# Latent attention of a two-layer trunk: TensorE in program order, in slots of two score tiles, with one batch of value products per unit

## The chip, the cores and the metric

The kernel is one program on one core of a Trainium2 chip. The metric is the device time of one execution in microseconds. The engines are TensorE (PE in the rows, PEld for its weight loads), VectorE (DVE), ScalarE (ACT), GpSimd (POOL) and SyncE (SP), which issues the DMAs.

## The reference

Two layers of a trunk run for two groups of tokens with the same weights: 128 prompt tokens, which attend among themselves, and 512 sample tokens, which attend to all sample keys and 128 cached ones. Each layer modulates its input, projects it, mixes it by three kinds of heads, projects the mixture out, and ends with a gated feed-forward part. Cut to what matters:

```python
def layer(x, cond, lp, layer_idx, ctx_cache):
    mod = jax.nn.silu(cond) @ lp["w_ada"] + lp["b_ada"]
    sh1, sc1, g1, sh2, sc2, g2 = jnp.split(mod.reshape((-1, 1, mod.shape[-1])), 6, axis=-1)
    ...
    y, new_ctx = mixers(x * (1.0 + sc1) + sh1, lp, lam, lam_init, ctx_cache)
    x = layer_norm(DEEPNORM_ALPHA * x + g1 * y, lp["ln1_g"], lp["ln1_b"])
    hf = x * (1.0 + sc2) + sh2
    f = (jax.nn.silu(hf @ lp["w_ff1"]) * (hf @ lp["w_ff3"])) @ lp["w_ff2"]
    x = layer_norm(DEEPNORM_ALPHA * x + g2 * f, lp["ln2_g"], lp["ln2_b"])

# in mixers: y_a a gated convolution, y_b differential attention (4 heads, two maps each), y_c:
    cq = rms_norm(m_cq, lp["q_norm_w"]);  qc = cq @ w_uq      # 8 heads of 64 + 32 (rotary)
    ckv = rms_norm(m_ckv, lp["kv_norm_w"])                     # sample: joined with the cached keys
    kv = ckv_all @ w_ukv                                       # 8 heads of 64 key + 64 value
    sc = jnp.einsum("bhqd,bhkd->bhqk", q_m, k_m) * MLA_SCALE   # q_m, k_m: 96 wide
    o_c = jnp.einsum("bhqk,bhkd->bhqd", jax.nn.softmax(sc, axis=-1), v_m)
    y = jnp.concatenate([y_a, y_b, y_c], axis=-1) @ w_out
```

## The kernel before

All 640 tokens (256 sample, 128 prompt, 256 sample) stand side by side as columns of tiles of 128 features. Large products are split into high and low parts in fp32r (three products each, `matmul3`, L344). A layer runs `stage_in` (input projection), `attention`, `stage_residual` (output projection), `stage_ff`.

Attention for the sample tokens is planned in `plan_steps` (L1383) as 64 steps, one score tile each: 128 queries of one head (and, in differential attention, one map) against 640 keys. Four differential units of eight tiles are followed by eight latent units (`mla_unit`, two heads by two query blocks, four tiles). `scores` (L1189) makes a tile: six products for a latent one (two for a differential one) into a PSUM buffer from `mm()`, the row maximum on VectorE (L1199), the exponential with its row sum on ScalarE (L1210), then the reciprocal (VectorE, L1248) and the scaling of P (GpSimd, L1249). `av_steps` (L1262) then makes the value products of a unit over five blocks of 128 keys: `tp(kt)` transposes the unit's four P tiles on TensorE (L1270) into a PSUM tile and copies it to an SBUF tile PT (L273 on ScalarE and L275 on VectorE in turn); `av(kt)` multiplies with the values into one accumulator from `ac()` (L1281). A dict `after` holds what follows a step: `put(i, f)` appends to step i. The value steps of a unit start `LAG` steps after its last score, and each step makes the next block's transposes and this block's value products. Side work is put there in the same way, by the tables at the head: loads of a pair of heads (`LOADS`, `load_pair`), the prompt's attention (`diff_prompt`, `mla_prompt`, as generators in two parts), the norm of the differential heads (`diff_norm`, three parts), all by `SIDE`, the split of finished rows (`split_y`), and in layer 0 the products that make later modulation vectors (`ada`, L491; `ada_pe` on TensorE for the first 24 calls, then `ada_pool`; `ada_finish` transposes the sum).

Steps 0 to 31 run between the jobs of the input projection and of the latent projections (`STEPS`, `JSTEPS`). The jobs are over then, and the rest, called here the last part, runs alone: `attention` (L1452) opens the PSUM stage "tr" and calls `step(1)` until all is done. PSUM there: two score buffers of two banks (`mm`), two banks "trx" for transposes, one bank "tr", one accumulator bank "ac".

The order of the program text isn't the order on the engines. A scheduler lays out each engine's queue from the dependencies and from predicted times, and takes an instruction that it holds to be ready ahead of an earlier one that isn't, unless a hint (`issue_after`) binds it. Each engine then works its queue off in that fixed order. Tiles of a pool are given out in turn, so that a new one waits until the old user of its buffer is done.

## Time and profile before

| what | value |
|---|---|
| median of 3 runs | 1757.66 us (1756.95 to 1759.01) |
| profiled execution | 1755.1 us |
| its span, first to last instruction | 1753.3 us |
| TensorE busy | 1697.4 us, 97% of the span |
| VectorE busy | 976.3 us, 56% |
| ScalarE busy | 614.0 us, 35% |
| GpSimd busy | 248.3 us, 14% |
| mean granted TensorE clock | 0.985 |

Times in the rows are microseconds from the start of the span, unless marked ns. A line such as L1195 is a line of the kernel; `out<-in` names its tiles. Matmuls overlap, so TensorE's busy time counts some of it twice. The chain of waits goes back from the end, at each step to what released the instruction, or to the one before it on its engine.

### The profile page before, as it was taken

What the parts mean: (1) busy time and instruction counts of PE and PEld (TensorE: products, weight loads), DVE (VectorE), ACT (ScalarE), POOL (GpSimd) and SP (SyncE); (2) the same over time, 40 slices, a digit from 0 to 9 for tenths busy, and PEclk for the clock granted to TensorE, in tenths of its full rate; (3) what the DMA queues carried; (4) which work ended last, traced back from release to release, by engine and by line L of the source; (5) the groups of instructions that cost most, each with busy time, mean ns of one, the idle gap of its engine ahead of it and who ended that gap; (6) DMA issues with size and microseconds to landing.
All of it is one profiled execution on the core that took longest, in us unless ns stands there. A gap on an engine that the chain in (4) does not pass through costs nothing.

```text
span 1753.3 us, 29480 instructions
## 1 busy us (share of the span) xinstructions
PE 1697.4 (97%) x11983; PEld 1587.8 (91%) x11983; DVE 976.3 (56%) x1824; ACT 614.0 (35%) x1046; POOL 248.3 (14%) x226
## 2 busy tenths in 40 slices
PE   8999989999999999999999999899999999999997
PEld 6998867698999999999999997678999999999997
DVE  3656777747466656756476668764652232232226
ACT  1334554524431122122245546554353212212221
POOL 0011113440001010101211111232300000000014
PEclk9999989999999999999999999899999999999998
DMA  9665584421354545545314634622212222222211
GB/s 335 207 200 142 170 253 130 127 84 55 103 148 148 156 132 147 172 128 151 103 52 142 218 121 158 179 73 78 73 61 75 82 73 73 69 79 82 68 53 60
DMA packets 100871, 217.38 MB, mean 124 GB/s; under 512 B 12160, under 2 KB 28928, under 8 KB 100736
## 3 DMA queue, kind: packets, MB, share of 16 engines
q1 hardware_dynamic: 100736, 215.50, 39.4%
q8 instruction: 94, 1.54, 0.4%
q14 instruction: 41, 0.34, 0.1%
HBM read 185.28 MB, written 30.18 MB: 123 GB/s over the span
## 4 chain that ended last, share of the span: by engine, by line
PE 85%; DVE 6%; DMA 3%; ACT 3%; issue 2%; SPq 0%; POOL 0%; POOLq 0%; ACTq 0%; DVEq 0%
PE mm L349 61%; PE mm L1195 4%; PE mm L372 4%; PE ac L1281 3%; PE mm L1514 3%; PE trx L1270 3%; PE mm L995 1%; DMA rawt<-in_w_ada 1%; PE mm L401 1%; DVE wu L140 1%; ACT hv L782 1%; DMA raw<-in_w_ada 1%; PE tr L449 1%; DMA mk<-kd 1%; ACT wu L138 1%
## 5 line engine op out<-in xcount | busy, mean ns | idle before, releaser
L349 PE MATMUL mm<-h,wu 128*128 128x384 f32 (+1 forms) x4944 | 736.0, 310 | 1.8 <-ACT kp L909 1.5
L349 PEld LDWEIGHTS mm<-h,wu 128*128 128x128 f32 x4944 | 724.7, 188 | 8.8 <-issue 5.4
L138 ACT CAST wu<-stg 128x1024 fp32r<-128x1024 f32 (+2 forms) x200 | 201.6, 1011 | 686.7 <-PE mm L349 334.1
L140 DVE TENSOR_TENSOR wu<-stg,wu 128x1024 fp32r<-128x1024 f32 (+2 forms) x200 | 239.4, 1200 | 157.5 <-ACT wu L138 155.2
L349 PE MATMUL mm<-gh,wu 128*128 128x256 f32 (+1 forms) x1184 | 258.7, 309 | 0.0
L349 PEld LDWEIGHTS mm<-gh,wu 128*128 128x128 f32 x1184 | 198.7, 188 | 0.9 <-issue 0.6
L349 PE MATMUL mm<-gl,wu 128*128 128x384 f32 (+1 forms) x592 | 182.8, 309 | 0.0
L1199 DVE TENSOR_REDUCE nm<-mm 128x1 f32<-128x640 f32 x128 | 104.8, 818 | 50.9 <-PE mm L1195 50.1
L1548 DVE TENSOR_TENSOR gs<-gs,mm 128x640 f32<-128x640 f32 (+2 forms) x48 | 36.6, 763 | 149.1 <-PE mm L349 149.1
L668 DVE SCALAR_TENSOR_TENSOR x<-mm,ga,x 128x512 f32<-128x512 f32 x48 | 36.0, 750 | 144.8 <-PE mm L349 144.8
L349 PEld LDWEIGHTS mm<-gl,wu 128*128 128x128 f32 x592 | 111.4, 188 | 0.2 <-issue 0.2
L527 DVE SCALAR_TENSOR_TENSOR acc<-rawt,scT,acc 128x512 f32<-128x512 f32 x98 | 75.6, 772 | 58.7 <-DMA rawt<-in_w_ada 57.5
L372 PE MATMUL mm<-h,wu 128*128 128x384 f32 (+1 forms) x576 | 98.1, 327 | 7.6 <-ACT h L783 6.9
L372 PEld LDWEIGHTS mm<-h,wu 128*128 128x128 f32 x576 | 90.7, 201 | 12.7 <-ACT h L783 9.6
L349 PE MATMUL mm<-hi,wu 128*128 128x384 f32 (+1 forms) x400 | 89.9, 311 | 0.1
L687 POOL TENSOR_TENSOR accS<-x 128x640 f32<-128x640 f32 x4 | 9.9, 2480 | 506.3 <-DVE x L674 506.3
L1195 PE MATMUL mm<-mk,mq 96*128 96x384 f32 (+1 forms) x384 | 74.9, 336 | 5.7 <-ACT P L1210 2.3
L532 DVE SCALAR_TENSOR_TENSOR rawt<-rawt,scT 128x512 f32<-128x512 f32 x98 | 74.8, 763 | 2.1 <-POOL rawt L525 2.1
L1195 PEld LDWEIGHTS mm<-mk,mq 96*128 96x128 f32 x384 | 63.7, 200 | 12.7 <-ACT P L1210 4.9
L349 PEld LDWEIGHTS mm<-hi,wu 128*128 128x128 f32 x400 | 67.9, 188 | 2.6 <-issue 1.5
L1210 ACT ACTIVATE P<-mm,nm 128x640 f32<-128x640 f32 x56 | 44.6, 796 | 57.1 <-DVE nm L1199 44.7
L525 POOL TENSOR_SCALAR acc<-rawt,scT 128x512 f32<-128x512 f32 x14 | 9.8, 697 | 373.7 <-PE tr L542 373.6
(272 smaller groups left out, 2250.2 us busy)
## 6 DMA issues: line engine op xcount, KB each, us to landing
stg<-in_w_ff SPq DMA_DIRECT2D x104, 512.0 KB, 3.6
rawt<-in_w_ada SPq DMA_DIRECT2D x160, 256.0 KB, 3.0
stg<-in_w_in SPq DMA_DIRECT2D x30, 512.0 KB, 4.2
stg<-in_w_ff SPq DMA_DIRECT2D x32, 448.0 KB, 3.3
raw<-in_w_ada SPq DMA_DIRECT2D x32, 256.0 KB, 6.2
stg<-in_w_out SPq DMA_DIRECT2D x16, 512.0 KB, 4.4
mk<-kd SPq DMA_DIRECT2D x32, 240.0 KB, 5.9
mq<-qd SPq DMA_DIRECT2D x32, 192.0 KB, 5.4
```

The costliest lines, as they stand in the source:

```text
L138: nc.scalar.copy(u[:, 0, :ncol], t[:, :ncol])
L140: (nc.gpsimd if self.lo_pool else nc.vector).tensor_sub(u[:, 1, :ncol], t[:, :ncol], u[:, 0, :ncol].bitcast(F32))
L349: self.last = nc.tensor.matmul(out, w(k, pw), x(k, px), start=(k == 0 and i == 0), stop=(k == nk - 1 and i == 2)).ins
L372: self.last = nc.tensor.matmul(ps, u[:, pw, 128 * k:128 * k + 128], x(k, px)[:, c0:c1], start=(k == 0 and i == 0), stop=(k == NK - 1 and i ...
L527: nc.vector.scalar_tensor_tensor(self.acc[0], w, c[0], self.acc[0], ALU.mult, ALU.add)
L532: nc.vector.scalar_tensor_tensor(self.acc[1], w, c[1], self.acc[1], ALU.mult, ALU.add)
L1195: nc.tensor.matmul(ps[:, 128 + c0:128 + c1], q[:96, qc:qc + 128], k[:96, c0:c1], start=(i == 0), stop=(i == len(pairs) - 1))
L1199: nc.vector.tensor_reduce(nm, s, axis=AX.X, op=ALU.max, negate=True)
L1210: self.exp_end = nc.scalar.activation(P, s, AF.Exp, bias=nm, accum_out=sm).ins
L1270: nc.tensor.transpose(p[:, 256 * i + 128 * q:256 * i + 128 * q + 128], tiles[i, q][:, 128 * kt:128 * kt + 128], self.ident)
L1281: nc.tensor.matmul(acc[64 * i:64 * i + 64, :256], v(kt, i), hold[kt][:, 256 * i:256 * i + 256], start=(kt == 0), stop=(kt == 4))
L1514: self.last = self.nc.tensor.matmul(ps[:, c0:c1], u[:, pw, 128 * k:128 * k + 128], x(k, px)[:, c0:c1], start=(k == 0 and j == 0), stop=(k ...
```

## The change

- From the stage "tr" on, TensorE's instructions are chained in the order of the program text: `in_order` binds each one to the one traced before it (an order, not a wait for its end).
- Steps run in slots: `slot` traces two score steps and then the side work put at either.
- From the last differential unit on, a unit's value products are one batch: transposes of blocks 0 and 1, then 2 and 3, then 4, at 2, 3 and 4 steps after its last score, and all value products at 5 steps. Before, they were five mixed steps from 4 steps on. For the earlier units the mixed steps stay, some one step earlier. Where no more `ada_pe` calls come, block 4 of a batch goes to the bank "tr".
- PT has six buffers instead of three.
- The prompt's parts are three instead of two (`prompt_out` yields before its value products), at new steps. Their scores and value products, and the scale product of `diff_norm`, go to the accumulator bank (its last block to "tr") instead of a score buffer.
- The prompt's operands (`p32`) are loaded by a step of their own, into one buffer instead of two.
- The `ada` calls stand at listed steps, and in this stage `ada_finish` follows two steps later.

The diff, with hunks of mere bookkeeping left out:

```diff
--- before.py
+++ after.py
...
@@ -56,8 +56,11 @@
 ADV = 0
 HOLD = 2
 LOADS = (29, 37, 43, 52)
-SIDE = ((34, 37), (37, 40, 43), (36, 40), (47, 50, 56), (44, 47), (49, 51), (51, 54), (60, 62))
-ADA_N = 12
+P32 = (38, 45, 49, 54)
+NPT = 6
+SIDE = ((32, 36, 38), (40, 43, 47), (36, 40, 42), (44, 47, 57), (44, 48, 50), (48, 52, 54), (52, 56, 58),
+        (60, 64, 66))
+ADA_AT = (32, 34, 38, 42, 44, 46, 50, 54, 58, 60, 62, 66)
 ADA_IN = 1
 ADA_PE = 6
 ADA_OUT = 2
@@ -315,6 +318,20 @@
             self.defer(n, fn)
         else:
             fn()
+
+    @contextmanager
+    def in_order(self):
+
+        traced, prev = self.nc.cur_bb.bb.instructions, self.pe_end
+        n = len(traced)
+        yield
+        for i in traced[n:]:
+            if i.engine == self.nc.tensor.engine:
+                if prev is not None:
+                    self.tc.add_manual_dep(i, prev.name, mybir.DependencyInfo(mybir.DependencyClass.NoSync,
+                                                                              mybir.DependencyReason.DATA))
+                prev = i
+        self.pe_end = prev
 
     def tick(self):
         for x in self.later:
@@ -510,7 +527,9 @@
             nc.vector.tensor_copy(self.ada_part, ps[:, :128])
         else:
             nc.vector.tensor_add(self.ada_part, ps[:, :128], self.ada_part)
-        if q == 3:
+        if q == 3 and self.kind == "tr":
+            self.after.setdefault(self.g + 2, []).append(lambda acc=self.ada_part: self.ada_finish(acc, key))
+        elif q == 3:
             self.ada_finish(self.ada_part, key)
 
     def ada_pool(self, key, q):
@@ -1183,8 +1202,11 @@
                 self.move(q[part][:96, :512], self.qd[r, :, part, :].rearrange("r i c -> (r i) c"))
                 self.move(k[part][:96, :], self.kd[r, :, part, :].rearrange("r i c -> (r i) c"))
             self.mq[h], self.mk[h] = q, k
-        self.p32[p] = self.at.tile([96, 2, 2, 128], F32, tag="p32", name="p32", bufs=2)
-        nc.sync.dma_start(self.p32[p], self.pd[64 * p:64 * p + 64].rearrange("(h r) i a c -> (r i) h a c", h=2))
+
+    def load_p32(self, p):
+
+        self.p32[p] = self.at.tile([96, 2, 2, 128], F32, tag="p32", name="p32", bufs=1)
+        self.nc.sync.dma_start(self.p32[p], self.pd[64 * p:64 * p + 64].rearrange("(h r) i a c -> (r i) h a c", h=2))
 
     def scores(self, pairs, qc):
 
@@ -1212,7 +1234,7 @@
 
     def pt(self):
         if self.at:
-            return self.at.tile([128, 512], F32, tag="PT", name="PT", bufs=3)
+            return self.at.tile([128, 512], F32, tag="PT", name="PT", bufs=NPT)
         return self.t(name="PTt")[:, 0:512]
 
     def diff_unit(self, l, p, hf):
@@ -1259,12 +1281,14 @@
             self.ys[2 + p] = self.t(name="yo")
         return self.ys[2 + p]
 
-    def av_steps(self, tiles, v, dst, hf):
+    def av_steps(self, tiles, v, dst, hf, batch):
+
+
         nc = self.nc
         hold = {}
 
         def tp(kt):
-            p = self.tr(True)
+            p = self.tr(not batch or kt < 4 or self.ada_i < 4 * ADA_PE)
             for i in range(2):
                 for q in range(2):
                     nc.tensor.transpose(p[:, 256 * i + 128 * q:256 * i + 128 * q + 128],
@@ -1291,6 +1315,9 @@
                 tp(kt + 1)
             av(kt)
 
+        if batch:
+            return [lambda kts=kts: [tp(kt) for kt in kts] for kts in ((0, 1), (2, 3), (4,))] + \
+                [lambda: [av(kt) for kt in range(5)]]
         return [lambda kt=kt: step(kt) for kt in range(5)]
 
     def soft_prompt(self, ps, n, neg=None):
@@ -1318,7 +1345,8 @@
         nc.tensor.transpose(p[:, 128:256], Pb, self.ident)
         pt = self.pt()
         self.copy(pt[:, :256], p[:, :256])
-        acc = p[:, 256:384]
+        yield
+        acc = self.ac()[:, 0:128]
         for i in range(2):
             nc.tensor.matmul(acc[64 * i:64 * i + 64, :], v(i), pt[:, 128 * i:128 * i + 128], start=True, stop=True)
         self.copy(dst[:, 256:384], acc)
@@ -1329,26 +1357,26 @@
         kv = km.rearrange("p (g t) -> p g t", g=4)
         nc.vector.tensor_mul(kv, self.kp32[:, p, :].unsqueeze(1).to_broadcast([128, 4, 128]),
                              self.block4.unsqueeze(2).to_broadcast([128, 4, 128]))
-        ps = self.mm()
+        ps = self.ac()
         nc.tensor.matmul(ps[:, :512], self.qp32[:, p, :], km, start=True, stop=True)
         P, Pv = self.soft_prompt(ps, 4, self.neglam[:, l:l + 1])
         yield
         h = Pv.rearrange("p (a b) t -> p a b t", b=2)
         nc.vector.tensor_add(h[:, :, 0, :], h[:, :, 0, :], h[:, :, 1, :])
-        self.prompt_out(P[:, 0:128], P[:, 256:384],
-                        lambda i: self.dvp[:, 128 * p + 64 * i:128 * p + 64 * i + 64], self.ob(p))
+        yield from self.prompt_out(P[:, 0:128], P[:, 256:384],
+                                   lambda i: self.dvp[:, 128 * p + 64 * i:128 * p + 64 * i + 64], self.ob(p))
         yield
 
     def mla_prompt(self, l, p):
         nc = self.nc
         x = self.p32[p]
-        ps = self.mm()
+        ps = self.ac()
         for i in range(2):
             nc.tensor.matmul(ps[:, 128 * i:128 * i + 128], x[:, i, 0, :], x[:, i, 1, :], start=True, stop=True)
         P, Pv = self.soft_prompt(ps, 2)
         yield
-        self.prompt_out(P[:, 0:128], P[:, 128:256],
-                        lambda i: self.vmp[:, 64 * (2 * p + i):64 * (2 * p + i) + 64], self.ob(2 + p))
+        yield from self.prompt_out(P[:, 0:128], P[:, 128:256],
+                                   lambda i: self.vmp[:, 64 * (2 * p + i):64 * (2 * p + i) + 64], self.ob(2 + p))
         yield
 
     def diff_norm(self, l, p):
@@ -1364,13 +1392,14 @@
         nc.vector.tensor_scalar(v, ps[:, :10], 1.0 / 64, 1e-6, ALU.mult, ALU.add)
         y = self.newton(v, 10)
         yield
-        pm = self.mm()
-        for j in range(5):
-            for i in range(2):
-                nc.tensor.matmul(pm[64 * i:64 * i + 64, 128 + 128 * j:256 + 128 * j],
-                                 y[:, 2 * j + i:2 * j + i + 1].to_broadcast([128, 64]), self.ident,
-                                 start=True, stop=True)
-        nc.vector.scalar_tensor_tensor(ob, ob, self.col("diff", l, 0), pm[:, 128:768], ALU.mult, ALU.mult)
+        for pm, j0, j1 in ((self.ac(), 0, 4), (self.tr(), 4, 5)):
+            for j in range(j0, j1):
+                for i in range(2):
+                    nc.tensor.matmul(pm[64 * i:64 * i + 64, 128 * (j - j0):128 * (j - j0) + 128],
+                                     y[:, 2 * j + i:2 * j + i + 1].to_broadcast([128, 64]), self.ident,
+                                     start=True, stop=True)
+            o = ob[:, 128 * j0:128 * j1]
+            nc.vector.scalar_tensor_tensor(o, o, self.col("diff", l, 0), pm[:, :128 * (j1 - j0)], ALU.mult, ALU.mult)
         yield
 
     def load_y(self, m):
@@ -1404,6 +1433,9 @@
         def unit(kind, p, hf, n):
             hold = {}
             g0 = len(self.steps)
+            end = g0 + n - 1
+            batch = end >= 31
+            at = (end + 2, end + 3, end + 4, end + 5) if batch else [end + LAG + (n * kt) // 6 for kt in range(5)]
 
             def start():
                 hold["u"] = kind(l, p, hf)
@@ -1416,12 +1448,12 @@
             def av(kt):
                 if kt == 0:
                     _, tiles, v, dst = hold["u"]
-                    hold["av"] = self.av_steps(tiles, v, dst, hf)
+                    hold["av"] = self.av_steps(tiles, v, dst, hf, batch)
                 hold["av"][kt]()
             for i in range(n):
                 self.steps.append(lambda i=i: step(i))
-            for kt in range(5):
-                put(g0 + n - 1 + LAG + (n * kt) // 5, lambda kt=kt: av(kt))
+            for kt, i in enumerate(at):
+                put(i, lambda kt=kt: av(kt))
 
         for kind, p, hf in units:
             unit(kind, p, hf, 8 if kind == self.diff_unit else 4)
@@ -1429,6 +1461,8 @@
             put(i, lambda g=g: self.assemble_diff(1, 2 * g, 2 * g + 2))
         for p, i in enumerate(LOADS):
             put(i, lambda p=p: self.load_pair(p))
+        for p, i in enumerate(P32):
+            put(i, lambda p=p: self.load_p32(p))
         parts(lambda: self.diff_prompt(l, 0), *SIDE[0])
         parts(lambda: self.diff_norm(l, 0), *SIDE[1])
         parts(lambda: self.diff_prompt(l, 1), *SIDE[2])
@@ -1438,8 +1472,8 @@
         put(54, lambda: self.load_y(0), lambda: self.load_y(1))
         for i, j in enumerate((58, 59, 56, 57, 58, 62)):
             put(j, lambda i=i: self.split_y(i))
-        for i in range(ADA_N):
-            put(32 + 2 * i, lambda: self.ada(1))
+        for i in ADA_AT:
+            put(i, lambda: self.ada(1))
 
     def step(self, n):
         for _ in range(n):
@@ -1448,6 +1482,16 @@
             for f in self.after.pop(self.g, []):
                 f()
             self.g += 1
+
+    def slot(self):
+
+        g = self.g
+        for f in self.steps[g:g + 2]:
+            f()
+        for i in (g, g + 1):
+            for f in self.after.pop(i, []):
+                f()
+        self.g += 2
 
     def attention(self, l):
         pool = self.tc.tile_pool(name="at", bufs=1, reuse_waits="tile")
@@ -1470,8 +1514,10 @@
             self.tick()
         self.W.lo_pool = False
         self.stage("tr")
+        self.pe_end = None
         while self.g < len(self.steps) or self.after:
-            self.step(1)
+            with self.in_order():
+                self.slot()
         self.split_y(6)
         self.split_y(7)
         self.stage("any")
```

## Rows read from the trace of the kernel before

**Rows 1.** The page, part 1: busy time, share of the span, instructions.

```profile
PE 1697.4 (97%) x11983; PEld 1587.8 (91%) x11983; DVE 976.3 (56%) x1824; ACT 614.0 (35%) x1046; POOL 248.3 (14%) x226
```

**Rows 2.** Busy time by stretch: PE, PEld, DVE, ACT, POOL; granted clock; DMA share, GB/s.

```profile
1107.30:1204.10 96.80, 93.10 (x662) 67.38 (x662) 65.72 (x152) 52.93 (x113) 34.31 (x40) 0.98 0.36 107
...
249.40:257.00 7.60, 6.61 (x34) 4.21 (x34) 2.47 (x6) 2.13 (x5) 1.60 (x2) 0.50 1.03 337
257.00:353.90 96.90, 94.19 (x773) 66.53 (x771) 69.82 (x168) 51.52 (x109) 35.67 (x40) 1.00 0.44 132
```

**Rows 3.** The chain of waits, layer 1: start, length, what; a score to value products.

```profile
1179.29 1.77 PE mm L1195 x12
1181.07 0.44 PE trx L1270 x4
1181.51 1.01 PE ac L1281 x8
1182.52 0.59 PE trx L1270 x4
...
1184.00 0.58 PE ac L1281 x4
```

**Rows 4.** Who waited for whom, layer 1, weight loads: in total, times, longest.

```profile
PEld trx L1270 <- issue: 13.5, 35, 0.4
```

**Rows 5.** The chain of waits, layer 1, pieces in its breaks.

```profile
1112.44 0.89 ACT P L1210 x2
...
1196.09 0.81 DVE lo L838
...
1197.14 0.81 POOL Pc L1249
...
1202.79 0.59 ACT PT L273
```

**Rows 6.** The chain of waits, layer 0: breaks, and one group of modulation products.

```profile
255.78 0.83 DVE nm L1199
...
295.57 0.57 PE tr L449 x16
...
318.62 2.79 DMA rawt<-in_w_ada
...
352.58 0.59 ACT PT L273
```

**Rows 7.** TensorE in order of time, layer 0: modulation products; idle before, releaser.

```profile
239.29 0.64 PE L449 MATMUL tr<-rawt,scT 128*32 128x128 f32 x16
...
251.98 0.65 PE L449 MATMUL tr<-rawt,scT 128*32 128x128 f32 x8 [0.99 <-DMA rawt<-in_w_ada]
```

**Rows 8.** The chain of waits, layer 1: prompt and norm work.

```profile
1118.91 0.87 PE mm L1333 x2
...
1122.48 0.37 PE tr L1323 x4
...
1156.23 0.45 PE mm L1347 x4
...
1157.84 1.01 PE tr L1362 x10
...
1175.87 1.24 PE mm L1370 x20
```

**Rows 9.** VectorE, layer 1, by line: busy us, mean ns, idle before, releasers.

```profile
L1199 DVE TENSOR_REDUCE nm<-mm 128x1 f32<-128x640 f32 x31 | 25.3, 817 | 5.6 <-PE mm L1195 5.1
L275 DVE COPY PT<-trx 128x512 f32<-128x512 f32 x18 | 12.4, 687 | 3.3 <-PE trx L1270 2.8 <-PE tr L1318 0.4
...
L275 DVE COPY yo<-ac 128x256 f32<-128x256 f32 x8 | 3.4, 425 | 4.0 <-PE ac L1281 3.9
```

**Rows 10.** The line that loads p32: issues on SP in ns, time to landing.

```profile
L1187 SPq DMA_DIRECT2D p<-pd x8: 317/327/414, 235.3 to 1156.7; - x8
...
DMA to landing us min/median/max: 2.4/2.9/6.7
```

More of the change, by code (lines that the diff above doesn't have):

```diff
@@ L1 @@
 import math
-from contextlib import ExitStack, nullcontext
+from contextlib import ExitStack, contextmanager, nullcontext
 import numpy as np
```

## The prediction

> **What bounds the kernel now.** I read the page first: TensorE is busy for 1697.4 of 1753.3 us [rows 1], so only what TensorE does, or waits for, can move the end. The change touches the latent part of attention, so I cut out of each layer the stretch in which that part runs alone: in layer 1 from the end of the second latent score tile (1108.96) to the first product of the output projection (1204.08), 95.1 us; in layer 0 from 249.5 to 353.9, 104.4 us. VectorE is busy for two thirds to three quarters of both, ScalarE for a little over half [rows 2]; TensorE bounds. By its busy time there seem to be only 3.7 us of headroom in layer 1. That time counts overlapping instructions, so I then read the chain of waits, which gives each piece once. There two score tiles of six products take 1.77 us, one block of four transposes 0.44 us behind scores but 0.59 us behind value products, and two value steps 1.01 us together but one alone 0.58 us [rows 3]. So going from transposes to value products costs 0.15 us, and the way back 0.16 us. The list of waits shows the latter from the side of the weight loads: 35 times a transpose's weights come late, with no releaser [rows 4].
>
> Then the breaks, where the chain leaves TensorE. Layer 1 has six (1.8, 1.6, 1.9, 1.1, 2.5 and 0.7 us), the first with the exponential at 1112.44, the longest with a split on VectorE at 1196.09 and GpSimd at 1197.14, the last with ScalarE's copy at 1202.79 [rows 5]; together 9.6. Each of the first four stands behind a prompt score or a norm's scale product, which had taken one of the two score buffers, so that the next score waited for the only other one's exponential. Layer 0 has six as well (1.8, 1.6, 1.9, 3.8, 2.5, 0.7), from the reduction at 255.78 to the copy at 352.58, with the one around the DMA of modulation weights at 318.62 [rows 6], plus 1.0 us of waiting for such weights at 251.98 [rows 7]; together 13.3.
>
> The work of layer 1 without changes of kind: 30 scores x 0.88 = 26.4; 45 transpose blocks x 0.43 = 19.4; 45 value steps x 0.43 = 19.4 [rows 3]; prompts and norms 2 x 0.87 + 4 x 0.45 + 12 x 0.11 + 6 x 0.37 + 2 x (1.01 + 1.24) = 11.6 [rows 8]; 0.7 for eight transposes at the lower clock. That is 77.5. The chain spends 95.1 - 9.6 = 85.5 on TensorE; the 8.0 left are the changes of kind (35 x 0.16 = 5.6 into transposes, the rest into value products).
>
> The Trainium skill ("Perfetto Trace Analysis", Identifying the Most-Contended Engine) says that TensorE's matmul busy share is no measure of headroom. By the busy share, 93.10 of 96.80 us [rows 2], this change could give 3.7 us there at most; by the chain 9.6 + 8.0. I go by the chain.
>
> **The change, part by part.**
>
> *One batch of value products per unit.* Per unit the sequence becomes transposes (2), (2), (1), then five value steps in a row. With nine such batches a layer (eight latent units and the last differential one) 9 x 0.15 + 9 x 0.16 = 2.8 us of changes stand where 8.0 stood: -5.2 us a layer, on the path, as TensorE bounds. The five transposed tiles of a unit now live at once, which six PT buffers hold; the prompt's masked keys take the next one and wait for the first value step, which comes early in a batch of 2.3 us.
>
> *Slots and program order.* Two score tiles, then the side work of two steps, and nothing of the stretch may pass: behind a waiting instruction stands everything that TensorE has here, and all other engines wait for that. A score buffer comes free 0.82 (reduction) + 0.89 (exponential and its sum) + some 0.2 of handovers = 1.9 us after its score ends [rows 5, 9]. A slot with value products covers this (2.3 + 1.0); one with three transpose blocks (1.3) just so, because the second score asks for its buffer 0.88 later; some 0.2 us are to spare. So a VectorE or ScalarE instruction that gets ahead of a reduction or an exponential shows. No row gives how often; the bounds are zero and one 0.69 us copy [rows 9] in each of 16 slots. I take the middle, 0.35 us a slot, as VectorE is busy for about two thirds: 5.6 us a layer, and keep 0 and 11 for the range.
>
> *Prompt in three parts, in the one accumulator bank.* No prompt score and no norm takes a score buffer any more, so the first four breaks go. In their place six prompt scores a layer ask for the accumulator just when a value batch has filled it: 0.42 for its copy [rows 9] plus 0.1 of handover, some 0.55 each, less 0.2 in the three slots where a prompt's transposes stand between: 2.7 us. The first norm's scale product puts its fifth block into the single "tr" bank, and the second norm's sums need that bank right behind: 0.9 us once. Splitting prompt_out lets its copy run a slot earlier: nothing on the path.
>
> *The end.* The last unit's transposes now come after the previous unit's last three blocks and value batch, 1.3 + 2.3 us; the last score's chain (1.9, then 0.16 and 0.81 on GpSimd, 3.0 with handovers) is covered by these. Of 2.5 + 0.7 us of breaks I keep 0.7.
>
> *The modulation work of layer 0.* Eleven product groups of 0.57 us [rows 6] run around this stage. Two the scheduler had put ahead of the stretch, where TensorE waited anyway (the second at 239.29 [rows 7]); chained behind the first latent scores they lose that cover: +1.1 us. The finishing transposition comes a slot later, and the calls stand further apart, so the 3.8 and the 1.0 us should go; if not, both stay.
>
> *Loads.* The p32 load leaves load_pair: one issue of 0.32 to 0.41 us [rows 10] less on SP, partly ahead of the first pair's loads, on which the first latent scores wait. Between 0 and -0.8 us in all; I take 0. With one buffer it waits for the prompt scores before it, and in SP's queue weights, modulation tiles and the next pair's loads wait behind it; it has two slots, some 10 us, against a landing in 2.4 to 6.7 us [rows 10], and costs the excess if that cover goes. *Earlier value steps of the differential units* (8*kt//6) lie beside projections; 1 us either way, taken as 0.
>
> *Sum.* Breaks after: 5.6 + 2.7 + 0.9 + 0.7 = 9.9 us a layer. Layer 1: 9.9 - 9.6 - 5.2 = -4.9. Layer 0: 9.9 - 13.3 - 5.2 + 1.1 = -7.5. Together -12.4. The profiled execution took 1755.1 us (span 1753.3), 2.6 below the median of the runs: 1742.7 in its terms, 1745 in the median's.
>
> **Rivals.**
>
> A. *The waits go too.* If the side work never delays a reduction, 5.6 us a layer more go, -11.2: 1734. For it: VectorE is idle a quarter to a third of the time. Against: the same 65.7 us of it [rows 2] will stand in some 90. Chance 0.17.
>
> B. *The modulation waits stay.* The 4.8 us of layer 0 remain, and as all else stands behind them in order, 2 more: 1752. For it: SP issues these loads in one queue with all others. Chance 0.08.
>
> C. *Waits in the slots eat it.* Break-even is 12.4 us over 32 slots, 0.39 us more in each, 0.74 in all: about one copy ahead of a reduction in every slot, 1756, no difference; chance 0.13. If a copy on each of the two engines is late (0.69 and 0.59) in two slots of three, that is 21 x (1.28 - 0.35) = 19.5 us, less the 12.4: 1765, slower. Its place is the slot with three transpose blocks. For it: at 1196.09 a split of 0.81 us ran on VectorE before the reciprocal that GpSimd and then TensorE waited for [rows 5]. Against: in the first four breaks the reduction itself came at once. Chance 0.08.
>
> D. *The clock.* TensorE was granted 0.50 of its clock, the 1.2 GHz level, for the 7.6 us after 249.4, behind a start full of waits; in the 96.9 us after that it kept 1.00, through breaks of up to 3.8 us [rows 2, 6]. If shorter but more frequent breaks brought it down, each such stretch would cost half its length, 3.8 us, and four a layer 30 us: 1775. Chance 0.04. The Trainium skill ("TensorE: Matmul & The Clock Gate", A second HAM failure mode) describes such a fall from short idle times between groups of products that cycle through PSUM banks. The 1.00 speaks against it here.
>
> **How the numbers follow.** The forecast (-7 to -18 us) has 0.50, A 0.17, B 0.08, C 0.13 and 0.08, D 0.04. About 0.2%, 3.5 us, is what a measurement of this kernel can tell from no change. So faster 0.75, same 0.13, slower 0.12. The range goes from near A's value (1735) to the upper end of "same" (1760): the slower cases and the lower half of A, some 0.2, lie outside.
>
> **What would show it.** In the chain of the changed kernel: value steps in pieces of 20 products and 2.3 us; late weights of transposes down from 35 to about 9 a layer; the stretch near 90 us in layer 1 and 97 in layer 0; breaks of about 0.5 us before prompt scores that end on a copy out of "ac"; a tail without the wait for GpSimd. Wrong would be: scores that wait for exponentials in most slots (C), a granted clock below 1.00 after the first 8 us (D), or a stretch of layer 0 that still waits for modulation weights (B).

## The result, and the profile after

| | before | after |
|---|---|---|
| median | 1757.6 us | 1773.6 us (1771.3 to 1774.6) |
| after / before | | 1.0092, interval 1.0079 to 1.0105 |
| profiled execution, span | 1755.1, 1753.3 us | 1771.3, 1769.5 us |
| mean granted clock | 0.985 | 0.979 |

The change makes the kernel 16 us slower, where 12 us faster were forecast. From the page of the kernel after, the span and parts 1 and 4 (busy time; the chain's share by engine):

```profile
span 1769.5 us, 29448 instructions
PE 1695.5 (96%) x11983; PEld 1598.3 (90%) x11983; DVE 975.2 (55%) x1828; ACT 614.6 (35%) x1046; POOL 247.1 (14%) x226
PE 85%; DVE 6%; ACT 4%; DMA 3%; issue 2%; POOL 0%; SPq 0%; POOLq 0%; ACTq 0%; DVEq 0%
```

The page shows hardly anything: the same 11983 TensorE instructions with nearly the same busy time as before [rows 1]. The difference lies in the two last parts. From here on a last part runs from the end of the second latent score tile to the last value product. Busy time by stretch (layer 0, layer 1; PE, PEld, DVE, ACT, POOL, then granted clock, DMA share and GB/s), first of the kernel before, cut to these bounds, then of the kernel after:

```profile
249.44:353.64 104.20, 100.50 (x805) 70.59 (x803) 72.25 (x174) 53.65 (x113) 37.26 (x42) 0.96 0.49 147
1108.69:1203.85 95.16, 91.47 (x658) 65.91 (x656) 65.55 (x150) 52.05 (x111) 34.13 (x40) 0.99 0.35 103
```

```profile
251.72:361.67 109.95, 100.47 (x852) 77.20 (x850) 71.32 (x177) 52.73 (x111) 35.65 (x42) 0.94 0.47 141
1117.67:1223.89 106.22, 96.56 (x673) 76.22 (x671) 65.25 (x153) 53.01 (x111) 33.97 (x40) 0.90 0.32 92
```

Layer 0's part is 5.8 us longer, layer 1's 11.1, and the granted clock is lower in both. Some 1.9 us of each are 11 products of the output projection that after begins earlier; without them it is 3.9 and 9.2. The remaining 3 us lie in the stages around these parts.

The first number behind the comma is TensorE's busy time. It counts time in which instructions overlap once, not twice: in layer 1 of the kernel before, the busy times of the single lines add up to 114 us, and the engine is busy for 91.5 of 95.2. So the difference is idle time, 3.7 us in either part before, 9.5 and 9.7 after. In layer 1 after it is mostly spent on these waits (who waits for whom, in total, times, longest); L1217 are the scores, L1375 and L1361 the prompt scores, L1390 the norms' sums:

```profile
PE mm L1217 <- ACT Pc L1232: 4.7, 5, 1.4
PE ac L1375 <- DVE yo L278: 1.4, 4, 0.5
PE ac L1361 <- DVE PT L1358: 0.9, 1, 0.9
PE tr L1390 <- DVE yo L1402: 0.9, 1, 0.9
PE tr L1390 <- ACT PT L276: 0.7, 1, 0.7
PE ac L1361 <- DVE yo L278: 0.5, 1, 0.5
```

The chain of waits of the kernel after in layer 1 (start, length, what) shows how a slot goes, and three kinds of loss:

```profile
1125.65 0.89 PE trx L1294 x8
1126.56 0.69 DVE PT L278
1127.32 0.73 DVE nm L1221
1128.14 0.89 ACT Pc L1232 x2
1129.08 1.14 PE mm L1217 x6
1130.22 2.33 PE ac L1305 x20
...
1138.77 0.60 PE tr L1294 x4
1139.45 0.52 ACT PT L276
1140.02 0.89 ACT Pc L1232 x2
1140.96 1.15 PE mm L1217 x6
...
1149.30 0.59 ACT PT L276
1149.93 1.28 PE tr L1390 x10
1151.21 2.83 PE mm L1217 x12
1154.04 2.92 PE ac L1305 x20
1156.98 0.44 DVE yo L278
1157.46 0.71 PE ac L1375 x4
1158.18 0.88 PE trx L1294 x8
1159.05 1.77 PE mm L1217 x12
```

First: at 1126.56 a copy of transposes runs on VectorE ahead of the row maximum, which then takes 0.73, the exponential 0.89, and only then do the next six score products run; at 1139.45 the copy ahead of the exponential is ScalarE's. Second: at 1149.30 TensorE waits for the one "tr" bank, and at 1156.98 for the accumulator bank. Third: the twelve score products at 1151.21 take 2.83 us instead of 1.77 and the value batch 2.92 instead of 2.33. The granted clock tells why. Stretches of the kernel after, same columns:

```profile
1149.93:1156.96 7.03, 7.00 (x42) 5.43 (x42) 3.90 (x15) 3.13 (x7) 2.07 (x3) 0.76 0.00 0
1164.27:1172.93 8.66, 8.66 (x43) 6.58 (x44) 3.62 (x15) 1.77 (x4) 2.40 (x3) 0.61 0.01 2
1202.78:1207.84 5.06, 5.03 (x26) 3.29 (x26) 3.09 (x7) 2.33 (x5) 3.06 (x4) 0.66 0.71 241
300.40:309.00 8.60, 8.54 (x42) 6.37 (x42) 3.34 (x14) 1.77 (x4) 1.52 (x2) 0.60 0.21 65
```

Three of the four begin with the two-column products of a norm's sums (five in the program, ten instructions in the trace), behind a wait; the other stands behind the casts that split finished rows, where the chain leaves TensorE for 5.2 us and TensorE itself waits for 1.4. The first norm's sums of layer 0, at 285.90, have no wait in front, and the scores and values behind them run at 1.00:

```profile
286.00:288.00 2.00, 2.00 (x16) 2.00 (x17) 0.84 (x5) 1.54 (x4) 0.80 (x1) 1.00 0.86 265
288.00:290.00 2.00, 2.00 (x18) 1.57 (x18) 1.62 (x7) 0.88 (x2) 0.00 (x0) 1.00 0.03 9
```

A share of 0.61 means that for much of the stretch the 1.2 GHz level was granted. Added up over the chain, the score and value pieces there are 6.5 us longer in layer 1 and 3.3 in layer 0 than at the 2.4 GHz level.

### The profile page after: what moved, and what is told of

It reads as the page before. It is cut to its first block, busy times and chain, and to the rows that moved or that the text cites. A ratio compares the mean times of both kernels' runs of the same rounds, so it can differ in the third digit from the quotient of the medians.

```text
span 1769.5 us, 29448 instructions
## 1 busy us (share of the span) xinstructions
PE 1695.5 (96%) x11983; PEld 1598.3 (90%) x11983; DVE 975.2 (55%) x1828; ACT 614.6 (35%) x1046; POOL 247.1 (14%) x226
## 4 chain that ended last, share of the span: by engine, by line
PE 85%; DVE 6%; ACT 4%; DMA 3%; issue 2%; POOL 0%; SPq 0%; POOLq 0%; ACTq 0%; DVEq 0%
PE mm L366 61%; PE mm L1217 4%; PE mm L389 4%; PE ac L1305 3%; PE mm L1560 3%; PE trx L1294 2%; PE mm L418 1%; DVE wu L143 1%; PE tr L1294 1%; PE mm L1014 1%; ACT wu L141 1%; PE ac L493 1%; ACT hv L801 1%; DMA mk<-kd 1%; PE tr L466 1%
## 5 line engine op out<-in xcount | busy, mean ns | idle before, releaser
L389 PE MATMUL mm<-h,wu 128*128 128x384 f32 (+1 forms) x576 | 95.1, 320 | 7.4 <-ACT h L802 6.8
L1217 PE MATMUL mm<-mk,mq 96*128 96x384 f32 (+1 forms) x384 | 76.5, 348 | 9.4 <-ACT Pc L1232 6.7
L1217 PEld LDWEIGHTS mm<-mk,mq 96*128 96x128 f32 x384 | 66.7, 211 | 13.6 <-ACT Pc L1232 8.7
```

Of the source, the lines that this page charges most:

```text
L389: self.last = nc.tensor.matmul(ps, u[:, pw, 128 * k:128 * k + 128], x(k, px)[:, c0:c1], start=(k == 0 and i == 0), stop=(k == NK - 1 and i ...
L1217: nc.tensor.matmul(ps[:, 128 + c0:128 + c1], q[:96, qc:qc + 128], k[:96, c0:c1], start=(i == 0), stop=(i == len(pairs) - 1))
```

## The experiments

Medians below are of each kernel's runs, each ratio is against the kernel before run beside it (medians of 1757.6 to 1758.6). The two columns on the right are the lengths of the last parts of the profiled execution with their granted clock, all from the view by stretch.

| kernel | median us | ratio, interval | layer 0 | layer 1 |
|---|---|---|---|---|
| before | 1757.6 | | 104.2, 0.96 | 95.2, 0.99 |
| after | 1773.6 | 1.0092 (1.0079 to 1.0105) | 110.0, 0.94 | 106.2, 0.90 |
| e1_free | 1759.2 | 1.0004 (0.9994 to 1.0013) | 101.4, 1.00 | 95.5, 0.98 |
| e3_late | 1790.5 | 1.0183 (1.0168 to 1.0198) | 117.4, 0.95 | 108.8, 0.91 |
| e4_norm | 1767.5 | 1.0047 (1.0031 to 1.0063) | 104.0, 0.97 | 99.5, 0.97 |
| e9_wide | 1768.9 | 1.0056 (1.0041 to 1.0071) | 106.8, 0.97 | 102.2, 0.95 |
| e6_mm | 1770.3 | 1.0070 (1.0049 to 1.0090) | 104.0, 0.98 | 103.4, 0.91 |
| e10_free_norm | 1764.0 | 1.0032 (1.0021 to 1.0044) | 103.0, 0.96 | 97.2, 0.96 |
| e13_three | 1758.1 | 0.9996 (0.9983 to 1.0010) | 100.5, 0.99 | 94.9, 0.98 |
| e15_split | 1757.7 | 0.9997 (0.9985 to 1.0009) | 100.7, 0.99 | 95.0, 0.98 |
| e5_batch | 1761.7 | 1.0021 (1.0010 to 1.0032) | 108.0, 0.95 | 95.1, 0.99 |
| e12_two | 1758.5 | 1.0002 (0.9988 to 1.0015) | 105.7, 0.95 | 94.7, 0.98 |
| e7_short | 1757.7 | 0.9994 (0.9983 to 1.0005) | 107.5, 0.95 | 93.9, 0.98 |
| e8_short_batch | 1751.6 | 0.9968 (0.9955 to 0.9981) | 104.2, 0.95 | 92.3, 0.99 |
| e8b_short_after | 1765.5 | 1.0041 (1.0024 to 1.0058) | 104.6, 0.96 | 101.9, 0.90 |
| e14_three_short | 1745.7 | 0.9928 (0.9909 to 0.9946) | 95.3, 0.99 | 89.2, 0.97 |

**The order alone taken back (e1_free).** The slots, the batches and the prompt's parts stay; only the binding of TensorE goes.

```diff
-            with self.in_order():
-                self.slot()
+            self.slot()
```

> The changed kernel without the chain of TensorE's instructions; slots, batches and the prompt's three parts stay. If strict order is what costs (nothing ready may pass a waiting instruction), the 21 us of breaks in layer 1 go back to some 10 and the clock stays up, so 1750 to 1758. If the cost lies in what stands in the queues of VectorE and ScalarE, or in the single accumulator and transpose banks, the time stays above 1767.

1759.2, just above the first bound: the strict order costs 14 us. But the free order doesn't give the batches: TensorE's weights for transposes of blocks come late, with no releaser, 24 times in layer 1's last part, against 35 before [rows 4] and 9 after (fifth blocks go to "tr"). The rows, e1_free and then after:

```profile
PEld trx L1294 <- issue: 7.2, 20, 0.6
PEld tr L1294 <- issue: 0.9, 4, 0.4
```

```profile
PEld trx L1294 <- issue: 1.7, 4, 0.6
PEld tr L1294 <- issue: 0.9, 5, 0.2
```

So order and batch belong together: in free order the batches of the text are in part taken apart again.

**The copies bound behind the scores (e3_late).** My first theory of the waits in the slots: copies of transposes and casts stand ahead of maxima and exponentials in VectorE's and ScalarE's queues, so bind them behind.

```diff
+            with self.late():      # issue_after(last traced maximum), issue_after(last traced exponential)
                 self.copy(pt, p)
...
+        with self.late():
             self.yh[m] = self.split(self.ys[m], f"y{m}")
```

> The changed kernel, with the copies of transposed tiles and the splits of finished rows bound behind the last traced score's reduction (on VectorE) and exponential (on ScalarE). If the queues are the cause (breaks that end on an exponential behind a copy or a cast: 2.5, 1.6, 1.5, 1.5 and 5.2 us in layer 1), about 12 us of breaks and the clock's fall after them go: 1752 to 1762. If strict order or the single banks are the cause, 1769 or more.

1790.5, 17 us slower than the kernel after. The queues do make the waits that they were blamed for: those of score products for exponentials fall from 4.7 to 2.4 us in layer 1, and the 2.1 us in layer 0 go. But the copies now come later, and TensorE's waits that end on a copy of a transposed tile rise from 1.0 to 5.9 us in layer 1 and from 2.3 to 9.8 in layer 0, most of them in front of work that needs the copied bank. In strict order all of TensorE stands behind these.

**The "tr" bank (e4_norm).** The fifth block of a batch always goes to "trx", and the second norm's sums stand two steps later.

```diff
-            p = self.tr(not batch or kt < 4 or self.ada_i < 4 * ADA_PE)
+            p = self.tr(True)
...
-SIDE = (..., (44, 47, 57), ...)
+SIDE = (..., (44, 49, 57), ...)
```

> The changed kernel, with the fifth block of a batch in the two-bank transpose ring instead of the single bank, and the second norm's sums one slot later than the first norm's scale product (step 49 instead of 47). If the single bank makes the waits of 0.65 and 0.9 to 1.1 us before the norm's sums, and these waits with the two-column sums behind them bring the clock down (1.7 and 3.3 us of slower work in layer 1, 3.3 in layer 0), some 10 us go: 1761 to 1765, and no stretch at 0.50 follows a norm. If the clock falls for another reason, the waits alone go: 1769 to 1772.

1767.5, 6 us better, between the two bounds; no stretch of the last parts shows the lower clock any more, apart from their beginning. TensorE no longer waits in front of a norm's sums. In layer 1 it is idle for longer than in the kernel after (11.6 against 9.7 us), so here more idle time alone doesn't bring the clock down.

**The clock alone (e9_wide).** Waits and order stay; each two-column product is made 128 columns wide, and the next one overwrites the surplus.

```diff
-            nc.tensor.matmul(ps[:, 2 * j:2 * j + 2], sq[:, 128 * j:128 * j + 128], self.block2, ...)
+            nc.tensor.matmul(ps[:, 2 * j:2 * j + 128], sq[:, 128 * j:128 * j + 128], self.wide2, ...)
```

> The kernel after, with the five two-column products of each norm's sums made 128 columns wide (the same two columns in front; each next product overwrites the rest). Order and waits stay. Theory 'narrow products behind a wait let the clock fall': no stretch at half clock behind the norm sums, and 1765 to 1769 instead of 1773.6. Rival 'the waits bring it down': the half-clock stretches stay and the time is 1773 to 1776 (some 0.1 us more for each wide product).

1768.9, the clock theory's upper end. The chain of e9_wide at the same place as 1149.30 to 1154.04 above, and its clock by stretch at the same two norms:

```profile
1150.54 0.59 ACT PT L276
1151.18 1.38 PE tr L1391 x10
1152.56 1.76 PE mm L1218 x12
1154.32 2.33 PE ac L1306 x20
```

```profile
1151.18:1156.65 5.47, 5.45 (x42) 4.29 (x42) 3.60 (x14) 2.57 (x6) 1.60 (x2) 1.00 0.00 0
1163.97:1169.45 5.48, 5.48 (x43) 4.39 (x44) 3.47 (x14) 1.15 (x3) 1.60 (x2) 1.00 0.01 3
```

The wait of 0.59 is the same, the norm's sums take 0.1 us more, and what follows runs at full clock. So behind the norms it is the narrow products together with the waits that bring the clock down: without the waits (e4_norm, and layer 0's first norm in the kernel after) or without the narrowness (e9_wide) it stays. The fall at the casts has no narrow products in front of it and is in e9_wide too:

```profile
1200.43 4.02 PE ac L1306 x20
```

In e4_norm TensorE waits nearly as long there (1.3 us), and the clock stays at 1.00. What makes the difference isn't settled. The last parts are 7.2 us shorter; layer 0's output projection gives 1.6 of that back.

**The accumulator bank (e6_mm).** The prompt's scores go back to the score buffers.

```diff
-        ps = self.ac()
+        ps = self.mm()
         nc.tensor.matmul(ps[:, :512], self.qp32[:, p, :], km, start=True, stop=True)
...
-        ps = self.ac()
+        ps = self.mm()
         for i in range(2):
             nc.tensor.matmul(ps[:, 128 * i:128 * i + 128], x[:, i, 0, :], x[:, i, 1, :], ...)
```

> The kernel after, with the prompt scores back in the score buffers instead of the accumulator bank. Theory 'accumulator waits' (seven waits of 0.5 us for the bank in the second layer's last part, as many in the first): 1767 to 1770. If those waits only stand in front of others that end as late: 1772 to 1775. Under strict order a score buffer taken for the prompts can hold up the next score tile: up to 1780.

1770.3, at the end of the first bound: worth 3 us, with an interval nearly as wide.

**All three (e13_three), and the "tr" edit in free order (e10_free_norm).** e13_three is the kernel after with the edits of e4_norm, e9_wide and e6_mm; e10_free_norm is e1_free with that of e4_norm.

> The kernel after, strict order and all, with e4_norm (bank and norm sums), e6_mm (prompt scores in the score buffers) and e9_wide (wide norm sums) together. Alone they gave about -6, -3 and -5 us against 1773.6. If they are three separate parts of what the strict order costs (14 us between e1_free and the kernel after): 1758 to 1762. If they mend the same waits and the same clock fall (e4_norm showed no half-clock stretch either): 1764 to 1768, no better than e4_norm alone.

1758.1: the three add up to 15.5 us, and strict order with them costs no more than free order without (e1_free 1759.2). The three in free order weren't run together.

> The kernel after without the strict order (e1_free) and with the fifth block's transposes always in their own bank and the norm sums two slots later (e4_norm). If the two mendings add up (1.0004 and, against 1773.6, -6 us): 1752 to 1755, faster than the kernel before. If the free order had already avoided those waits, as the absence of half-clock stretches in e1_free suggests: 1757 to 1761.

1764.0, above both bounds: with e4_norm's edit the scheduler laid the free order out anew, with the lower clock back at two places. Why isn't settled.

**The batches alone (e5_batch, e12_two).** The kernel before with the batches and five PT buffers; and the same in two batches of two and three blocks.

```diff
+            batch = end >= 31
+            at = (end + 2, end + 3, end + 4, end + 5) if batch else [end + LAG + (n * kt) // 5 for kt in range(5)]
...
+        if batch:
+            return [lambda kts=kts: [tp(kt) for kt in kts] for kts in ((0, 1), (2, 3), (4,))] + \
+                [lambda: [av(kt) for kt in range(5)]]
```

> The kernel before with one edit of the change: from the last differential unit on, transposes in three groups and one batch of value products per unit (five PT buffers instead of three); order, single steps and the prompt stay. If the changes between transposes and value products cost what the chain shows (0.15 and 0.16 us each), the batches give -8 to -11 us: 1747 to 1750. If batches cost as much in late value products and held buffers, 1756 or more.

> The kernel e5_batch (the batches alone, free order) with each unit's value products in two batches (two blocks, then three) instead of one. Theory 'two chains': a batch in two parts leaves value products to fill TensorE while a score tile waits for its maximum, and still saves half of the switches; 1753 to 1757. If the batches lose for another reason (the copies of the transposes come in bursts either way): 1759 to 1763, as e5_batch.

1761.7, by its second bound, and 1758.5, between its two bounds: no gain either way. Late weights of transposes fell only to 15 (e5_batch, layer 1): the batches are in part taken apart here too. The kernel before with the strict order alone, or with the slots alone, wasn't run, so what either costs by itself isn't shown.

**The score chain out of the way.** If the batches' saving is real, something as long as TensorE's work must hide it. The candidate is the chain of a score tile: products, row maximum, exponential, buffer free. A one-column multiplication takes the place of the row maximum, in the kernel before (e7_short), with the batches alone (e8_short_batch) and in the kernel after (e8b_short_after).

```diff
-        nc.vector.tensor_reduce(nm, s, axis=AX.X, op=ALU.max, negate=True)
+        if self.kind == "tr":
+            nc.vector.tensor_scalar(nm, s[:, 0:1], 0.0, None, ALU.mult)
+        else:
+            nc.vector.tensor_reduce(nm, s, axis=AX.X, op=ALU.max, negate=True)
...
```

> The kernel before, with the row maximum of every score tile from the modulation stage on replaced by a one-column multiplication by zero on VectorE (and a smaller scale in the exponential so that nothing overflows): VectorE still stands between the score products and the exponential, but for well under 0.3 us instead of 0.82. It leaves out the row maxima. If the score chain (products, maximum, exponential, buffer free) sets part of the end beside TensorE, the breaks of 9.6 and 13.3 us in the two last parts shrink and the time falls to 1735 to 1750; if the last parts were TensorE's alone, TensorE's own pieces (85 us in the second layer) stay and the time is within 4 us of 1758.

> The same short maximum on the kernel that has only the batched value products (e5_batch). To be read against e7_short, as e5_batch is read against the kernel before (there +4 us). Theory 'two chains': the batches' saving on TensorE was real and was lost because the score chain is as long as TensorE's work; with the chain out of the way the batches gain 6 to 10 us over e7_short. Rival 'batches cost as much': whatever the chain, batching makes its own waits (copies of the transposes in bursts, buffers), and this run is within 2 us of e7_short or up to 5 us slower.

> The kernel after (slots, strict order, batches, prompt work in three parts) with the same one-column stand-in for the row maximum from the modulation stage on; it leaves out the row maxima. The short maximum was worth nothing on the kernel before (e7_short 0.9994) and about 10 us on the batches alone (e8_short_batch 1751.6 against 1761.7). Theory 'strict order makes TensorE wait out the score chain in every slot': at least as much here, 1755 to 1762, and the breaks in the two last parts (24.3 and 21.0 us) fall to under 14 each. Rival 'the order's loss is the clock, the accumulator bank and the modulation work': 1766 to 1772, half-clock stretches still there.

VectorE's groups in layer 1's last part of e7_short (mean ns of one behind the busy time) show that the stand-in takes 153 ns instead of 817 [rows 9]:

```profile
L1200 DVE TENSOR_SCALAR nm<-mm 128x1 f32<-128x1 f32 x31 | 4.7, 153 | 10.7 <-PE mm L1195 9.6 <-POOL Pc L1252 0.7
```

The kernel before doesn't gain by it (0.9994): its last parts are TensorE's, as the prediction said. With the batches it is worth 10 us (1761.7 to 1751.6), and the batches are then worth 6 us over e7_short, the lower bound of the theory. But TensorE's busy time hardly falls with them (in layer 1 from 91.5 us in e7_short to 91.4, with 20 late weights of transposes left); what falls is its idle time, from 2.4 to 0.9. So this pair doesn't show a saving on TensorE. In the kernel after it is worth 8 us and the lower clock stays (0.90 in layer 1), between the two expectations: there the three faults are still in.

**The two together (e14_three_short).** The strict order, mended, with the stand-in.

> e13_three (strict order with the three mendings) with the one-column stand-in for the row maximum; it leaves out the row maxima. If the mended order costs nothing more, it comes where the batches alone came with the short maximum (e8_short_batch 1751.6): 1748 to 1753, so some 5 to 10 us under e13_three, and the size that was predicted for the change (1745) is reached but for a few us. If strict order still costs something of its own: 1755 to 1758.

1745.7, below the first bound. That makes a table of four, each in us:

| | row maximum over 640 columns | one-column stand-in |
|---|---|---|
| order and steps of before | 1757.6 (before) | 1757.7 (e7_short) |
| the change, three faults mended | 1758.1 (e13_three) | 1745.7 (e14_three_short) |

Either step alone gives nothing, both give 12 us, as where two chains of nearly the same length run side by side, TensorE's and that of the scores, and taking from one leaves the other. The last parts say the same: in layer 1 the chain of waits is off TensorE for 40 of 94.9 us in e13_three, where that was 9.6 before. Stretches of e13_three, then of e14_three_short:

```profile
252.39:352.87 100.48, 93.48 (x841) 72.88 (x839) 71.09 (x177) 52.66 (x111) 35.64 (x42) 0.99 0.52 155
1111.02:1205.87 94.85, 86.83 (x662) 69.04 (x660) 64.72 (x155) 54.02 (x113) 34.43 (x40) 0.98 0.36 103
```

```profile
251.54:346.80 95.26, 92.26 (x841) 72.56 (x839) 52.54 (x177) 53.31 (x111) 36.07 (x41) 0.99 0.53 162
1106.21:1195.40 89.19, 86.28 (x662) 69.11 (x660) 46.75 (x153) 53.47 (x111) 34.23 (x39) 0.97 0.39 111
```

In layer 1 TensorE is busy 86.8 us in e13_three, 4.6 less than before, but idle for 8.0 of 94.9, where it was idle for 3.7 of 95.2. In e14_three_short it is busy for nearly the same, 86.3, and idle for 2.9. What score products (L1218) and transposes wait for in e13_three (in total, times, longest) and in e14_three_short:

```profile
PE mm L1218 <- ACT Pc L1233: 3.9, 5, 1.4
PE trx L1295 <- ACT PT L276: 2.6, 3, 1.0
```

```profile
PE trx L1298 <- ACT PT L276: 0.7, 3, 0.2
PE mm L1218 <- ACT Pc L1236: 0.3, 1, 0.3
```

The stand-in shortens the score chain and also takes 18 us of work off VectorE in each layer. Which of the two frees TensorE, the latency or the shorter queue, these runs don't tell apart. The latency of the score tiles alone isn't that long: 0.88 + 0.82 + 0.89 us and 0.2 of handovers [rows 3, 5, 9] with two buffers allow a tile every 1.4 us, an estimate of 42 us for 30 tiles. The rest of that chain would be other work in the queues of VectorE and ScalarE; e3_late points to it, no run isolates it.

**The casts (e15_split).** In e13_three the chain leaves TensorE for 14 us from 1183.12 on, at the casts of `split_y` and the maxima and exponentials behind them.

```diff
-        for i, j in enumerate((58, 59, 56, 57, 58, 62)):
+        for i, j in enumerate((60, 64, 54, 58, 56, 62)):
```

> e13_three with the six casts that split the attention outputs spread over steps 54 to 64 (one every second step) instead of 56 to 62 in pairs. In e13_three the chain leaves TensorE for 14 us at the casts, maxima and exponentials of 1183 to 1197. If the casts ahead of the exponentials end last there: 1753 to 1756, and that break falls under 8 us. If the chain only runs beside TensorE there: 1757 to 1760.

1757.7, no change: the chain then leaves TensorE at other places instead. A stretch of the chain off TensorE isn't TensorE's idle time; where two chains are equally long it goes by either.

## Why the prediction was wrong

Forecast were 1745 and a range of 1735 to 1760; it became 1773.6, a miss of 28.6 us. The step that failed first is "I go by the chain". The sum struck off the breaks of the chain before, 9.6 and 13.3 us, as time that TensorE could win. But a break of the chain isn't idle time: TensorE worked beside it, and was idle for only 3.7 us in either part. (The prediction had set this number aside because busy time counts overlap; it counts it once.) The waits put in their place were right in size. The second step is the clock, for which the sum had nothing. Layer 1 in the prediction's terms, in us:

| term | forecast | measured |
|---|---|---|
| breaks before, taken as gone | -9.6 | -3.7 (idle before) |
| waits after: for exponentials, in the slots | 5.6 | 4.7 |
| accumulator bank | 2.7 | 2.8 |
| "tr" bank | 0.9 | 1.6 |
| end | 0.7 | 0.6 |
| changes of kind | -5.2 | -3.3 (rest of the busy time) |
| lower clock | 0 | 6.5 |
| sum | -4.9 | 9.2 |

In layer 0 the same two steps failed: idle before was 3.7, not 13.3, and the lower clock cost 3.3. Breaks and clock together are 25.3 of the 28.6 us; some 3 lie outside the last parts.

The runs say what can be had back. The three faults of the strict order cost 15.5 us (after to e13_three): the falls of the clock, and some idle time (9.7 to 8.0 us in layer 1). That still gives no gain over before, because the score chain takes what TensorE gives up; with the stand-in 12.4 us more go (e13_three to e14_three_short). That the two add up to nearly 28.6 is chance: e14_three_short does less work than the kernel that was forecast, and some waits of the faults were in the sum.

- **The switches: size about right, place wrong.** Value batches of 20 products took 2.33 us at full clock and late weights of transposes fell from 35 [rows 4] to 9, as forecast; TensorE's busy time in layer 1 fell by 4.6 us in e13_three where -5.2 was forecast. "On the path, as TensorE bounds" held only by a hair: in e13_three idle time rose by 4.3 us at the same time. The prediction had the chain of one score tile (1.9 us) and found it covered in a slot; it never asked how long that chain is over the whole part.
- **The waits in the slots.** 5.6 us a layer were forecast; TensorE's waits for exponentials are 4.7 us in layer 1 and 2.1 in layer 0. From e13_three to e14_three_short the last parts lose 5.2 and 5.7 us. Rival C's place was right too: the slot with three transpose blocks is the one at 1138.77, where ScalarE's copy stands ahead of the exponential, and two more like it follow. A stretch of 90 us in layer 1 was forecast with these waits and those for the banks in it, so some 81 without. In e14_three_short, which has hardly any of them, it has 89.2, and TensorE is busy for 86.3 of these: 81 was out of reach there, for the same reason, the breaks before taken as gone.
- **The accumulator.** Breaks of 0.5 us, ending on the copy out of "ac" (1156.98), came as described, five of them in layer 1, and a longer one. Taking the prompt's scores out gave 3 us in all, less than these waits in both layers.
- **The "tr" bank.** Forecast was one wait of 0.9 us a layer. In layer 1 it came twice: 0.7 us at 1149.30, for the copy of a fifth block, and 0.9 us ahead of the second norm's sums at 1164.27, as forecast, for the scale product's bank, whose reader on VectorE stood behind a copy and a row maximum; in layer 0 once, 1.0 us ahead of 300.46, besides 2.6 us at modulation work for the same bank. The worse effect was on the clock behind it.
- **The clock (rival D).** Given a chance of 0.04 and 1775 us, it is the rival whose effect was seen, though not by frequent breaks alone, as it had put it; that 1775 lies so near the measured time is chance, as the clock alone doesn't cost that much. Before, 1.00 held through breaks of 3.8 us [rows 2, 6], and the prediction took that for the whole case. But those were breaks of the chain too: in layer 1 before, no single wait of TensorE is longer than 1.2 us. And it hadn't asked what stands behind the break. Behind a wait and a norm's two-column products the 1.2 GHz level was granted, three times; e9_wide puts the price at about 5 us (7.2 in the last parts), far below the 30 that the rival was given. The Trainium skill ("TensorE: Matmul & The Clock Gate", A second HAM failure mode) puts such a fall down to frequent short idle times of TensorE between groups of products, in a kernel that cycles through PSUM banks. This case's trace agrees that short waits between groups take part in it (0.59 us at 1149.30), but not that they suffice: e9_wide has the same wait and a clock of 1.00.
- **Modulation (rival B).** Not seen as put: no wait of TensorE in the kernel after ends on a load of modulation weights, where 1.0 us did before [rows 7]. The chain of layer 0 still leaves TensorE at modulation work from 347.78 to 355.27, and for 7.6 us from 341.10 in e13_three; TensorE itself is idle for 2.4 of the 7.5 us.
- **Earlier steps and loads.** Taken as 1 us either way; the jobs before the last parts took 1.3 and 1.9 us more. No run tested which edit does that.

Both forecasts of the whole, faster and 1745, thus failed on the same reading: breaks of a chain were taken for idle time of the busiest engine, in the sum and in the argument against the clock, and the chain beside TensorE was costed for one tile only.

## What to carry to other kernels

A break in the chain of waits isn't idle time of the busiest engine: before counting it as time to win, read that engine's idle time in the same stretch. Before costing work taken off that engine, find out how long the next chain beside it is: replace its longest step by a short stand-in, in the kernel as it is and in the changed one, and read the table of four. A wait in a strict program order can cost twice, once by itself and once by what TensorE does behind it, so look for single banks and narrow products there first. A batch written into the text need not be one on the engine: here it was only where the order was bound.

## What was not expected of the hardware

A norm's five fp32 products of two columns each (ten instructions, 1.28 us) behind a wait of 0.7 to 1.0 us were followed by 3 to 7 us at the 1.2 GHz level: twelve score products took 2.83, 3.40 and 3.19 us instead of 1.77. Widened to 128 columns, they took 1.38 us, hardly more, and the granted clock behind them stayed at 1.00. Two columns wide without a wait, it stayed at 1.00 too.
